# A 27,000-instruction transformer kernel on one core: mean one tile sooner, weight refills one by one at two mixers, sign-flipped logits, more background steps

## The chip, the core and the metric

The kernel runs on one core of a Trainium2 chip. TensorE (PE) multiplies 128-row tiles into PSUM, VectorE (DVE) and ScalarE (ACT) do elementwise work, GpSimd (POOL) a few elementwise operations, SyncE (SP) issues most DMAs. The metric is the device time of one execution in microseconds (us), median of several runs.

## What is computed

Two blocks, 256 tokens of width 1024, all in float32. The first puts 16 meta tokens in front (272 tokens) and runs two layers of SwiGLU, mixer, SwiGLU; the mixer is a neighborhood attention (16 heads), then a differential attention (8 heads). The second is a hybrid layer: causal attention (8 heads; with 256 tokens MoBA's own block is all there is) beside an mLSTM (4 heads), one output projection, then a squared-ReLU MLP.

```python
h = h + 0.5 * rmsnorm(swiglu(rmsnorm(h, g[0]), ...), g[1])
h = h + rmsnorm(mixer(rmsnorm(h, g[2])), g[3])
h = h + 0.5 * rmsnorm(swiglu(rmsnorm(h, g[4]), ...), g[5])
# differential attention, per head
p = softmax(q @ k.T + bias)              # two maps
o = rmsnorm((p[0] - lam * p[1]) @ v, subln_g) * (1 - lambda_init)
# hybrid layer
ig = mi + b_igate;  lf = log_sigmoid(mf + b_fgate)
hm = rmsnorm(mlstm(q, k, v, ig, lf)) * g * sigmoid(mo)
x = x + rmsnorm(concat(att, hm) @ w_out, g_mix_post)
x = x + rmsnorm(square(relu(rmsnorm(x) @ w_up)) @ w_down, g)
```

## The kernel before

**Products.** Activations lie transposed, features on partitions and tokens along the row, 8 blocks of 128 features. Every float32 product is made of three: x and w are split into a high half and a low half (the rest), and `mm3` (L387 to L389) multiplies xh·wh, xl·wh, xh·wl. `gemm` does that for the 8 blocks k of one output tile of 128 columns, 24 products; `inside` is a table of functions to be called after block k, and after the blocks in `bg_at[0]` it calls `bg()`, one step of a background generator.

**Weights.** `Weights` keeps a ring of 7 split tiles. `high` makes the high half on ACT (L150), `low` subtracts it on DVE (L162); a raw buffer holds two tiles, and its second `low` lets SP load the next. `pump(n)` does up to n lows (of tiles whose high half was ordered before) and n highs, as far as the ring has room. Engines run their instructions in the order in which the code was written, so a pump's place is its place in both queues.

**Phase start.** `start_phase` needs four weight tiles at once, multiplies them with an unnormalized x, sums the squares of h on DVE (`norm.sum`, L441 to L443), and ends with `pump(2)`. The factor 1/rms comes later: `Norm.steps` puts `head` (row sums on PE at L338, a small DVE row at L350, a power on POOL) after block 0 of the second tile behind the start, and `tail` (transposes, then ACT's copy `rb`, L456) after block 3. The first of these two tiles waits in PSUM as `p2`. Evacuations multiply by `rb`.

**Mixers.** `mixer` writes 20 such tiles behind the start, (value, then query, key, value for three groups), each followed by its evacuation, `W.pump()` and `bg()`, with `bg_at` at blocks 2 and 5. The background is an attention generator: per unit u `scores` (PE products, then `softmax` on DVE and ACT), `weights` (division by the sum), `turn` (transposes two units later), `turn_v` every second unit, `values`. Score and product tiles share six PSUM buffers, transposes have two. The hybrid layer has its own loop over `plan`, and three generators in turn: `gates`, `mlstm`, `causal_attention`. What is left of them at the end runs inside `proj_out`, two steps per block.

Of the kernel before, what the change touches and what calls it, by code (L numbers as in the profile page):

```python
# [20 lines left out]
NM = 16  # L21
# [182 lines left out]
def block_kernel(ctx: ExitStack, tc: tile.TileContext, a, out):  # L204
# [254 lines left out]
    def start_phase(norm, post, n=4):  # L459
# [43 lines left out]
        W.low_if()  # L503
        W.done(n)
        W.pump(2)
        return ps

    def first_phase(norm, feed, n=4):
# [69 lines left out]
        W.low()  # L578
# [4 lines left out]
        W.pump(2)  # L583
        W.pump(2)
# [52 lines left out]
    def ffn(norm, post, before, start=start_phase):  # L637
# [20 lines left out]
        for n in range(1, NF // 2):  # L658
            for q in range(2):
                p = ps_mm()  # L660
                if n == 1 and q == 0:
                    p2 = p
                    gemm(p, norm.x, c)
                    continue
                elif n == 1:
                    gemm(p, norm.x, c, inside=norm.steps)
# [239 lines left out]
    def softmax(ps, parts, n):  # L906

        lg, mx = tmp("lg"), -3.0e38
# [8 lines left out]
        return e, sm  # L917
# [32 lines left out]
    def na_attention():  # L950
# [8 lines left out]
        def scores(u):  # L959
# [5 lines left out]
            s0 = 2 - 2 * qt  # L965
            for b in range(2):
                hd = 2 * hp + b
                bias = bt[hp // 2][:, hd % 4, s0:s0 + 4, :].rearrange("p s k -> p (s k)")
                P[u, b] = softmax(ps[b], [(slice(0, NM), mb[:, hd * NM:hd * NM + NM]), (GRID, bias)], T)

        def weights(u):
            for b in range(2):
                e, sm = P[u, b]
                r = small([128, 1])
                dve.reciprocal(r, sm)
                dve.tensor_scalar(e, e, r, None, op0=OP.mult)
                P[u, b] = e
# [97 lines left out]
    def mixer(norm, post, evac, attention, q_cols, before):  # L1075
# [6 lines left out]
        for n, part, st in [(n,) + x for n, x in enumerate(  # L1082
                [(2, 0)] + [(part, st) for st in range(1, 4) for part in (0, 1, 2)])]:
            c = q_cols if part == 0 else norm.cols
            for q in range(2):
                before(2 * n + q)
                p = ps_mm()
                gemm(p, norm.x, c, inside=norm.steps if n == 0 and q else {})
                if n == 0 and q == 0:
                    p2 = p  # L1090
                    continue
# [8 lines left out]
                W.pump()  # L1100
# [68 lines left out]
    def da_attention():  # L1169
        vp, A, AT, OS, normed = {}, {}, {}, {}, {}  # L1170

        def scores(u):
            hd, qt = divmod(u, 2)
            A[u] = []
            for s in range(2):
# [4 lines left out]
                A[u].append(softmax(ps, [(ALL, t5b[hd // 4][:, hd % 4, u0:u0 + T])], T))  # L1180

        def weights(u):
            (e0, s0), (e1, s1) = A[u]
            r0, r1 = small([128, 1]), small([128, 1])
# [5 lines left out]
            A[u] = e0  # L1190
# [10 lines left out]
        def values(u):  # L1201
# [5 lines left out]
            m, r = small([128, 1]), small([128, 1])  # L1207
            dve.tensor_scalar(m, ss, 1.0 / 128, EPS, op0=OP.mult, op1=OP.add)
            pool.tensor_tensor(r, m, mhalf[:, 0:1], op=OP.pow)
            normed[u] = o, r  # L1210

        def scale(u):
            hd, qt = divmod(u, 2)
            o, r = normed.pop(u)
            if qt == 0:
                OS[hd] = keep()
            dve.tensor_scalar(OS[hd][:, qt * 128:qt * 128 + 128], o, r, None, op0=OP.mult)
# [74 lines left out]
    def gates():  # L1292
# [47 lines left out]
    def mlstm():  # L1340
# [57 lines left out]
        for u in range(8 + 4):  # L1398
# [17 lines left out]
            yield  # L1416

# [37 lines left out]
    def causal_attention():  # L1455
# [3 lines left out]
        def scores(u):  # L1459
# [3 lines left out]
            for b in range(2):  # L1463
                s = slice(64 * b, 64 * b + 64)
                pe.matmul(ps[b][:, 0:n], qk[s, hp, QT[qt]], qk[s, 4 + hp, NM:NM + n], start=True, stop=True)
            for b in range(2):
                lg, mx = tmp("lg"), small([128, 1])
                dve.tensor_tensor_reduce(out=lg[:, 0:n], in0=ps[b][:, 0:n], in1=causal[:, 256 - n:256], scale=1.0,
                                         scalar=-3.0e38, op0=OP.add, op1=OP.max, accum_out=mx)
                nmx = small([128, 1])  # L1470
                dve.tensor_scalar(nmx, mx, -0.125, None, op0=OP.mult)
                e, sm = keep(), small([128, 1])
                act.activation(e[:, 0:n], lg[:, 0:n], AF.Exp, bias=nmx, scale=0.125, accum_out=sm)
                P[u, b] = e, sm

        def weights(u):
            n = 128 * (u % 2 + 1)
            for b in range(2):
                e, sm = P[u, b]
                r = small([128, 1])  # L1480
                dve.reciprocal(r, sm)
                dve.tensor_scalar(e[:, 0:n], e[:, 0:n], r, None, op0=OP.mult)
# [44 lines left out]
    for n, (kind, i) in enumerate(plan):  # L1527
# [3 lines left out]
        gemm(p, norm.x, c, inside=norm.steps if n == 1 else {})  # L1531
        if n == 0:
            p2 = p
            continue
# [39 lines left out]
    for f in range(4, 32):  # L1574
        p = ps_mm()
        gemm(p, norm.x, c, inside=norm.steps if f == 5 else {})
        if f == 4:
            p2 = p
            continue
# [101 lines left out]
```

## Time and profile before

| | us |
|---|---|
| median of 3 runs | 1453.06 (1451.36 to 1454.84) |
| the profiled execution | 1454.09 |
| its span | 1452.3 |
| PE busy | 1422.2 (98%) |
| DVE busy | 927.7 (64%) |
| ACT busy | 753.2 (52%) |
| mean granted clock | 0.993 |

The first mixer lies at about 228 to 345 us, the second at 798 to 910, the hybrid layer's at 1121 to 1245. In a row of the timeline the first number is the start, the second how long the row took (rows of several instructions are merged), and the bracket says how long the engine stood idle before and what ended that.

### The profile page before, as it was taken

Reading aid. Unit: us, or ns where it says so; the run is one execution under the profiler, and the core shown is the slowest. Engines: PE = TensorE matmul, PEld = TensorE weight load, DVE = VectorE, ACT = ScalarE, POOL = GpSimd, SP = SyncE. Lnnn points to the kernel's source line nnn. Section 1 sums busy time; section 2 is a strip of 40 time slices with the busy share of each in tenths; the row PEclk is TensorE's granted clock in tenths of the full one; section 3 lists DMA queues with packets and bytes.
Section 4 is the critical chain, followed back from the end, with each engine's and each line's share of the span. In section 5 each row is a group of like instructions: output and inputs, shape, how many; then the busy total and the mean of one; then the engine's idle time right before and its main releaser. Section 6 shows DMA issues by size and latency. Waiting matters only on the chain.

```text
span 1452.3 us, 27152 instructions
## 1 busy us (share of the span) xinstructions
PE 1422.2 (98%) x11092; PEld 1365.1 (94%) x11092; DVE 927.7 (64%) x1852; ACT 753.2 (52%) x1331; POOL 154.3 (11%) x149
## 2 busy tenths in 40 slices
PE   9999999999999999999999899999999999999997
PEld 9999998788999999999999799999999888999886
DVE  6767448874775544865545777686644878686542
ACT  6554446665654444554444556564444565676541
POOL 1314000100021100121100011021200000000000
PEclk9999999999999999999999999999999999999999
DMA  8896555431475555365553433275554443265650
GB/s 267 259 254 181 184 167 138 110 117 59 140 254 174 168 189 167 117 204 174 177 172 117 145 117 116 88 232 177 192 190 140 142 149 116 88 213 195 211 180 29
DMA packets 230025, 236.40 MB, mean 163 GB/s; under 512 B 17857, under 2 KB 220390, under 8 KB 229710
## 3 DMA queue, kind: packets, MB, share of 16 engines
q1 hardware_dynamic: 228702, 229.36, 49.6%
q0 software_dynamic: 656, 4.94, 1.2%
q8 instruction: 87, 1.43, 0.4%
q10 hardware_dynamic: 544, 0.38, 0.1%
q14 instruction: 36, 0.29, 0.1%
HBM read 233.60 MB, written 5.13 MB: 164 GB/s over the span
## 4 chain that ended last, share of the span: by engine, by line
PE 71%; DVE 4%; ACT 1%; issue 0%; POOL 0%; DVEq 0%; POOLq 0%; ACTq 0%
PE pm L387 19%; PE pm L389 18%; PE pm L388 18%; PE ps L1604 2%; PE ps L1603 2%; PE ps L1605 2%; PE pm L500 2%; PE pm L496 1%; DVE wl L162 1%; PE pm L497 1%; PE ps L1205 1%; PE ps L1177 1%; PE pt L338 1%; DVE hb L615 0%; DVE xh L480 0%
## 5 line engine op out<-in xcount | busy, mean ns | idle before, releaser
L162 DVE TENSOR_TENSOR wl<-wr,wh 128x1024 fp32r<-128x1024 f32 (+1 forms) x430 | 516.2, 1208 | 119.5 <-ACT wh L150 118.7
L387 PE MATMUL pm<-xh,wh 128*128 128x272 f32 (+1 forms) x1992 | 583.8, 293 | 2.2 <-ACT ring L986 1.2
L389 PE MATMUL pm<-xh,wl 128*128 128x272 f32 (+1 forms) x1992 | 571.6, 287 | 0.0
L388 PE MATMUL pm<-xl,wh 128*128 128x272 f32 (+1 forms) x1992 | 570.2, 286 | 0.0
L150 ACT ACTIVATE wh<-wr 128x1024 fp32r<-128x1024 f32 (+1 forms) x430 | 441.0, 1033 | 196.9 <-PE pm L388 117.7
L387 PEld LDWEIGHTS pm<-xh,wh 128*128 128x128 f32 x1992 | 377.5, 190 | 15.8 <-issue 11.0
L388 PEld LDWEIGHTS pm<-xl,wh 128*128 128x128 f32 x1992 | 377.4, 189 | 0.1
L389 PEld LDWEIGHTS pm<-xh,wl 128*128 128x128 f32 x1992 | 377.4, 189 | 0.0
L389 PE MATMUL pm<-mh,wl 128*128 128x272 f32 (+1 forms) x704 | 202.3, 287 | 0.0
L387 PE MATMUL pm<-mh,wh 128*128 128x272 f32 (+1 forms) x704 | 202.1, 287 | 0.0
L388 PE MATMUL pm<-ml,wh 128*128 128x272 f32 (+1 forms) x704 | 201.6, 286 | 0.0
L648 POOL TENSOR_TENSOR sr<-sl,rb 128x272 f32<-128x272 f32 (+1 forms) x88 | 106.9, 1219 | 318.9 <-ACT sl L646 318.9
L389 PEld LDWEIGHTS pm<-mh,wl 128*128 128x128 f32 x704 | 132.7, 189 | 0.0
L387 PEld LDWEIGHTS pm<-mh,wh 128*128 128x128 f32 x704 | 132.6, 188 | 0.0
L388 PEld LDWEIGHTS pm<-ml,wh 128*128 128x128 f32 x704 | 132.6, 188 | 0.0
L414 ACT ACTIVATE mh<-m 128x272 fp32r<-128x272 f32 (+1 forms) x88 | 37.7, 429 | 122.8 <-DVE m L653 122.7
L653 DVE TENSOR_TENSOR m<-pm,sr 128x272 f32<-128x272 f32 (+1 forms) x88 | 38.3, 435 | 79.4 <-PE pm L389 75.5
L644 DVE TENSOR_TENSOR gq<-pm,rb 128x272 f32<-128x272 f32 (+1 forms) x88 | 37.6, 435 | 74.7 <-PE pm L389 66.8
L646 ACT ACTIVATE sl<-gq 128x272 f32<-128x272 f32 (+1 forms) x88 | 36.9, 427 | 92.3 <-DVE gq L644 92.0
L343 POOL TENSOR_TENSOR s<-s,mhalf 128x3 f32<-128x3 f32 (+1 forms) x15 | 11.9, 793 | 607.7 <-DVE s L356 356.6
L382 DVE TENSOR_TENSOR accf<-accf,sq 128x272 f32<-128x272 f32 (+1 forms) x42 | 18.3, 435 | 82.5 <-ACT sq L381 82.4
L916 ACT ACTIVATE keep<-lg,s 128x272 f32<-128x272 f32 x64 | 33.5, 523 | 48.2 <-DVE s L914 47.8
(337 smaller groups left out, 1801.8 us busy)
## 6 DMA issues: line engine op xcount, KB each, us to landing
wr<-in_ffn_w_gate_dram SPq DMA_DIRECT2D x43, 1024.0 KB
wr<-in_ffn_w_up_dram SPq DMA_DIRECT2D x43, 1024.0 KB
wr<-in_ffn_w_down_dram SPq DMA_DIRECT2D x32, 1024.0 KB
wr<-in_w_up_dram SPq DMA_DIRECT2D x16, 1024.0 KB
wr<-in_w_down_dram SPq DMA_DIRECT2D x16, 1024.0 KB
wr<-in_ffn_w_down_dram SPq DMA_DIRECT2D x16, 768.0 KB
wr<-in_na_w_qkv_dram SPq DMA_DIRECT2D x12, 1024.0 KB
wr<-in_da_w_qkv_dram SPq DMA_DIRECT2D x12, 1024.0 KB
```

The costliest lines, as they stand in the source:

```text
L150: self.nc.scalar.activation(hi, w, AF.Copy)
L162: engine.tensor_tensor(lo, w, hi.bitcast(F32), op=OP.subtract)
L387: pe.matmul(ps, wh[:, k, :], xh[:, j, cols], start=start, stop=False)
L388: pe.matmul(ps, wh[:, k, :], xl[:, j, cols], start=False, stop=False)
L389: pe.matmul(ps, wl[:, k, :], xh[:, j, cols], start=False, stop=stop)
L414: act.activation(hi, src, AF.Copy)
L500: pe.matmul(ps[q][:, c], w[q][0][:, k, :], norm.xl[:, k, c], start=False, stop=k == 7)
L644: dve.tensor_tensor(t[:, c], ps[:, c], norm.rb[:, c], op=OP.mult)
L646: act.activation(s[:, c], t[:, c], AF.Silu)
L648: pool.tensor_tensor(s2[:, c], s[:, c], norm.rb[:, c], op=OP.mult)
L653: dve.tensor_tensor(t[:, c], ps[:, c], gated.pop(f)[:, c], op=OP.mult)
L916: act.activation(e[:, 0:n], lg[:, 0:n], AF.Exp, bias=nmx, accum_out=sm)
```

## The change

In the `order` rows below numbers behind a name tell buffers apart.

*Mean sooner.* `head` moves to block 3 of the first tile behind a phase start (`norm.first`), `tail` to block 1 of the second. `start_phase` loses its second `low_if` and `pump(2)`; the callers pump after the first tile instead: 2 in the feed-forward phases and the hybrid layer, 1 in `mixer`. In `mixer` later tiles pump 1, and 2 only in the second tile of a step from the fourth step (n >= 3).

*Softmax.* The logits are written with the opposite sign and their minimum is taken, which serves as the exponential's bias with scale -1; the operation that negated the maximum goes. Both sums of a unit lie in one tile, and one reciprocal takes them. In the differential attention e0 is no longer scaled: e0 + e1·x with x = -lam·s0/s1, and 1/s0 enters in the row norm and in `scale`.

*Steps.* `gates` has two more `yield`s around the log-sigmoid, `mlstm` two before its last head.

```diff
-            self.steps = {0: self.head, 3: self.tail}
+            self.first, self.second = {3: self.head}, {1: self.tail}
...
         norm.sum(squares)
-        W.low_if()
         W.done(n)
-        W.pump(2)
         return ps
...
-        W.low()
         norm.sum(squares)
         for _ in range(n):
             W.next()
         W.done(n)
-        W.pump(2)
-        W.pump(2)
+        W.pump(1)
...
-            lo, mx = mx, small([128, 1])
-            dve.tensor_tensor_reduce(out=lg[:, cols], in0=ps[:, cols], in1=bias, scale=1.0, scalar=lo,
-                                     op0=OP.add, op1=OP.max, accum_out=mx)
-        nmx = small([128, 1])
-        dve.tensor_scalar(nmx, mx, -1.0, None, op0=OP.mult)
-        e, sm = keep(), small([128, 1])
-        act.activation(e[:, 0:n], lg[:, 0:n], AF.Exp, bias=nmx, accum_out=sm)
+            hi, mn = mn, small([128, 1])
+            dve.tensor_tensor_reduce(out=lg[:, cols], in0=ps[:, cols], in1=bias, scale=-1.0, scalar=hi,
+                                     op0=OP.add, op1=OP.min, accum_out=mn)
+        e = keep()
+        act.activation(e[:, 0:n], lg[:, 0:n], AF.Exp, bias=mn, scale=-1.0, accum_out=sm)
...
         def weights(u):
+            r = small([128, 2])
+            dve.reciprocal(r, P.pop(u))
             for b in range(2):
-                e, sm = P[u, b]
-                r = small([128, 1])
-                dve.reciprocal(r, sm)
-                dve.tensor_scalar(e, e, r, None, op0=OP.mult)
...
-                gemm(p, norm.x, c, inside=norm.steps if n == 0 and q else {})
+                gemm(p, norm.x, c, inside=(norm.first, norm.second)[q] if n == 0 else {})
                 if n == 0 and q == 0:
                     p2 = p
+                    W.pump(1)
                     continue
...
-                W.pump()
+                W.pump(2 if n >= 3 and q else 1)
...
-            dve.reciprocal(r0, s0)
-            dve.reciprocal(r1, s1)
-            dve.tensor_scalar(e0, e0, r0, None, op0=OP.mult)
-            dve.tensor_tensor(r1, r1, nlam, op=OP.mult)
-            dve.scalar_tensor_tensor(e0, e1, r1, e0, op0=OP.mult, op1=OP.add)
+            dve.reciprocal(r, sm)
+            dve.scalar_tensor_tensor(x, r[:, 1:2], sm[:, 0:1], nlam, op0=OP.mult, op1=OP.mult)
+            dve.scalar_tensor_tensor(e0, e1, x, e0, op0=OP.mult, op1=OP.add)
...
-            dve.tensor_scalar(m, ss, 1.0 / 128, EPS, op0=OP.mult, op1=OP.add)
+            dve.scalar_tensor_tensor(m, ss, r0, r0, op0=OP.mult, op1=OP.mult)
+            dve.tensor_scalar(m, m, 1.0 / 128, EPS, op0=OP.mult, op1=OP.add)
...
         yield
         yield
+        yield
         dve.scalar_tensor_tensor(f, f, 0.0, w[32:36, :], op0=OP.min, op1=OP.subtract)
+        yield
         yield
...
                 scale(u - 3)
             yield
+            if u == 10:
+                yield
+                yield
...
         if n == 0:
             p2 = p
+            W.pump()
             continue
```

DVE's queue in the first mixer, before, from the weights of unit 0 (reciprocals, scaling of the exponentials `keep`) over one tile's evacuation (`qkv`, product tile `pm` times `rb`) to the first logits of unit 1. `wl` is a weight tile's low half, `lg` the logits, `s` small tiles:

```order
L975 RECIPROCAL s_2916<-s_2896 128x1
L976 TENSOR_SCALAR keep_2569<-keep_2569,s_2916 128x272
L975 RECIPROCAL s_2919<-s_2905 128x1
L976 TENSOR_SCALAR keep_2569<-keep_2569,s_2919 128x272
L934 TENSOR_TENSOR qkv_2928<-pm_2875,rb_2825 128x272
L162 TENSOR_TENSOR wl_2865<-wr_2758,wh_2864 128x1024
L162 TENSOR_TENSOR wl_2871<-wr_2758,wh_2870 128x1024
L911 ISA lg_2945,s_2946<-ps_2941,mb 128x16
L911 ISA s_2946 128x1
L911 ISA lg_2945,s_2948<-ps_2941,bt_1139,s_2946 128x256
L911 ISA s_2948 128x1
L914 TENSOR_SCALAR s_2950<-s_2948 128x1
```

The same stretch now:

```order
L971 RECIPROCAL s_2901<-s_2879 128x2
L974 TENSOR_SCALAR keep_2569<-keep_2569,s_2901 128x272 x2
L930 TENSOR_TENSOR qkv_2911<-pm_2865,rb_2815 128x272
L162 TENSOR_TENSOR wl_2843<-wr_2508,wh_2842 128x1024
L909 ISA lg_2923,s_2924<-ps_2918,mb 128x16
L909 ISA s_2924 128x1
L909 ISA lg_2923,s_2926<-ps_2918,bt_1139,s_2924 128x256
L909 ISA s_2926 128x1
L909 ISA lg_2929,s_2930<-ps_2919,mb 128x16
```

One `wl` of the tile is gone, so is the `TENSOR_SCALAR s<-s` behind the logits, and one reciprocal of two columns stands where two stood.

DVE's queue at the gates of the hybrid layer, before, from the evacuation of the tile behind the gates' (`vt`) to the copy of the transposed gates (`gi`); `vtok` holds the gate rows here, and L1303 is the log-sigmoid's last step:

```order
L1427 TENSOR_TENSOR vt_13570<-pm_13804,rb_13827 128x256
L162 TENSOR_TENSOR wl_13768<-wr_13482,wh_13767 128x1024
L162 TENSOR_TENSOR wl_13771<-wr_13482,wh_13770 128x1024
L1303 SCALAR_TENSOR_TENSOR vtok_13571<-vtok_13571 4x256
L1427 TENSOR_TENSOR vt_13570<-pm_13863,rb_13827 128x256
L162 TENSOR_TENSOR wl_13855<-wr_13758,wh_13854 128x1024
L162 TENSOR_TENSOR wl_13861<-wr_13758,wh_13860 128x1024
L1308 COPY gi<-pt_13900 128x72
```

And now:

```order
L1431 TENSOR_TENSOR vt_13362<-pm_13603,rb_13613 128x256
L162 TENSOR_TENSOR wl_13595<-wr_13274,wh_13594 128x1024
L162 TENSOR_TENSOR wl_13601<-wr_13274,wh_13600 128x1024
L1431 TENSOR_TENSOR vt_13362<-pm_13655,rb_13613 128x256
L162 TENSOR_TENSOR wl_13647<-wr_13550,wh_13646 128x1024
L162 TENSOR_TENSOR wl_13653<-wr_13550,wh_13652 128x1024
L1303 SCALAR_TENSOR_TENSOR vtok_13363<-vtok_13363 4x256
L1431 TENSOR_TENSOR vt_13362<-pm_13692,rb_13613 128x256
L162 TENSOR_TENSOR wl_13683<-wr_13598,wh_13682 128x1024
L162 TENSOR_TENSOR wl_13689<-wr_13598,wh_13688 128x1024
L1309 COPY gi<-pt_13728 128x72
```

The log-sigmoid stands behind one more evacuation and two more low halves, and from it to the copy of `gi` the same three instructions stand.

PE's queue inside the hybrid layer's output projection, before, from the last scores of the causal attention (`ps<-qk`) on; `pm<-Oh` and `pm<-Ol` are the projection's products:

```order
L1465 MATMUL ps_15141<-qk_13569 128x256
L1465 MATMUL ps_15142<-qk_13569 128x256
L387 MATMUL pm_15006<-Oh_13567,wh_14570 128x256
L388 MATMUL pm_15006<-Ol_13568,wh_14570 128x256
L389 MATMUL pm_15006<-Oh_13567,wl_14571 128x256
L387 MATMUL pm_15007<-Oh_13567,wh_14648 128x256
L388 MATMUL pm_15007<-Ol_13568,wh_14648 128x256
L389 MATMUL pm_15007<-Oh_13567,wl_14649 128x256
L387 MATMUL pm_15008<-Oh_13567,wh_14698 128x256
```

And now, from the last scores on; `ps<-ring,vtok` are the values of the last but one pair of heads, `pt<-ident` transposes:

```order
L1469 MATMUL ps_14908<-qk_13361 128x256
L1469 MATMUL ps_14909<-qk_13361 128x256
L1503 MATMUL ps_14925<-ring_13560,vtok_13363 64x128 x6
L1338 MATMUL pt_14933<-ident,vt_13362 128x128 x2
L1494 MATMUL pt_14937<-ident,vtok_13363 128x128
L1494 MATMUL ps_14940<-ident,mq_13364 128x128
L387 MATMUL pm_14723<-Oh_13359,wh_14338 128x256
L388 MATMUL pm_14723<-Ol_13360,wh_14338 128x256
L389 MATMUL pm_14723<-Oh_13359,wl_14339 128x256
```

Twelve products followed the last scores before (seven stand here); now the values follow them. Further on the last values of all were followed by 24 products of this kind, 12 for another head pair and then 12 for their own; now by their own 12 alone.

## Rows read from the trace of the kernel before

**Rows 1.** The page, part 1: engine, busy us, share, instructions.

```profile
PE 1422.2 (98%) x11092; PEld 1365.1 (94%) x11092; DVE 927.7 (64%) x1852; ACT 753.2 (52%) x1331; POOL 154.3 (11%) x149
```

**Rows 2.** PE's waits: for whom, total us, times, longest.

```profile
PE pt L985 <- ACT bt L892: 3.3, 4, 2.2
...
PE ps L1015 <- DVE s L911: 1.9, 2, 1.3
PE pt L1391 <- DVE mq L1385: 1.8, 1, 1.8
...
PE pm L387 <- ACT ring L986: 1.2, 1, 1.2
```

**Rows 3.** Windows: length, PE busy, granted clock (1.00 is 2.4 GHz), DMA.

```profile
246.00:256.00 10.00, 6.89 (x45) 0.83 0.80 219
266.00:271.00 5.00, 2.79 (x21) 1.00 0.70 218
819.00:832.00 13.00, 7.86 (x39) 0.74 0.51 163
1000.00:1025.00 25.00, 25.00 (x213) 1.00 0.61 199
1149.00:1157.00 8.00, 7.28 (x39) 0.57 0.79 254
```

**Rows 4.** Timeline of PE, first mixer: scores of units 1 and 2.

```profile
242.42 0.73 PE L964 MATMUL ps<-kq 64*128 64x272 f32 x4
...
247.16 0.73 PE L964 MATMUL ps<-kq 64*128 64x272 f32 x4
```

**Rows 5.** Timeline of DVE, first mixer: one tile, with unit 1.

```profile
245.72 0.43 DVE L934 TENSOR_TENSOR qkv<-pm,rb 128x272 f32<-128x272 f32 x1
246.07 2.35 DVE L162 TENSOR_TENSOR wl<-wr,wh 128x1024 fp32r<-128x1024 f32 x2
248.34 0.17 DVE L911 CUSTOM_DVE_ANT_0 lg<-ps,mb 128x16 f32<-128x16 f32 x1
...
250.72 0.17 DVE L975 RECIPROCAL s<-s 128x1 f32<-128x1 f32 x1 [0.21 <-ACT keep L916]
...
251.19 0.43 DVE L934 TENSOR_TENSOR qkv<-pm,rb 128x272 f32<-128x272 f32 x1
```

**Rows 6.** Timelines of POOL and DVE: a bias mask and what lay beside it.

```profile
255.27 3.47 POOL L776 TENSOR_TENSOR bt<-bt,misc 128x1536 f32<-128x1536 f32 x1 [19.00 <-DMA bt<-rpb_rows]
...
255.97 2.84 DVE L1021 TENSOR_TENSOR lm<-lm,mx 16x64 f32<-16x64 f32 x1
```

**Rows 7.** Timeline of DVE, second mixer: one tile, with unit 1.

```profile
815.57 0.42 DVE L1155 SCALAR_TENSOR_TENSOR kq<-pm,rb 128x256 f32<-128x256 f32 x1
...
820.02 0.16 DVE L1186 RECIPROCAL s<-s 128x1 f32<-128x1 f32 x1 [0.38 <-ACT keep L916]
...
820.97 0.42 DVE L1155 SCALAR_TENSOR_TENSOR kq<-pm,rb 128x256 f32<-128x256 f32 x1
```

**Rows 8.** Timeline of PE, second mixer: scores of units 1, 2; values of 0.

```profile
813.34 0.73 PE L1177 MATMUL ps<-kq 64*128 64x272 f32 x4
...
817.44 0.73 PE L1177 MATMUL ps<-kq 64*128 64x272 f32 x4
...
825.72 1.65 PE L1205 MATMUL ps<-vs,ring 128*128 128x128 f32 x6 [5.14 <-ACT vs L891]
```

**Rows 9.** Timeline of PE, hybrid layer: gate transposes, cumulative sums.

```profile
1147.91 0.28 PE L1307 MATMUL pt<-ident,vtok 36*128 36x36 f32 x2 [2.22 <-DVE vtok L1303]
...
1150.78 0.56 PE L1311 MATMUL pt<-gi,misc 128*128 128x4 f32 x2 [0.72 <-DVE gi L1308]
```

**Rows 10.** Timeline of DVE, hybrid layer: log-sigmoid; last low half of attention.

```profile
1147.35 0.41 DVE L1303 SCALAR_TENSOR_TENSOR vtok<-vtok 4x256 f32<-4x256 f32 x1
...
1244.16 0.42 DVE L415 TENSOR_TENSOR Ol<-ps,Oh 128x256 fp32r<-128x256 f32 x1 [2.83 <-ACT Oh L414]
```

**Rows 11.** Timeline of PE, hybrid layer: the last values.

```profile
1242.83 0.88 PE L1501 MATMUL ps<-ring,vtok 128*64 128x128 f32 x12
```

More of the change, by code (lines that the diff above doesn't have):

```diff
@@ L662, in ffn @@
                     p2 = p
-                    gemm(p, norm.x, c)
+                    gemm(p, norm.x, c, inside=norm.first)
+                    W.pump(2)
                     continue
                 elif n == 1:
-                    gemm(p, norm.x, c, inside=norm.steps)
+                    gemm(p, norm.x, c, inside=norm.second)
                     gate(ps4[0], 0)
@@ L965, in scores @@
             s0 = 2 - 2 * qt
+            sm = small([128, 2])
             for b in range(2):
@@ L968, in scores @@
                 bias = bt[hp // 2][:, hd % 4, s0:s0 + 4, :].rearrange("p s k -> p (s k)")
-                P[u, b] = softmax(ps[b], [(slice(0, NM), mb[:, hd * NM:hd * NM + NM]), (GRID, bias)], T)
+                P[u, b] = softmax(ps[b], [(slice(0, NM), mb[:, hd * NM:hd * NM + NM]), (GRID, bias)], T, sm[:, b:b + 1])
+            P[u] = sm
         def weights(u):
+            r = small([128, 2])
+            dve.reciprocal(r, P.pop(u))
             for b in range(2):
-                e, sm = P[u, b]
-                r = small([128, 1])
-                dve.reciprocal(r, sm)
-                dve.tensor_scalar(e, e, r, None, op0=OP.mult)
-                P[u, b] = e
+                e = P[u, b]
+                dve.tensor_scalar(e, e, r[:, b:b + 1], None, op0=OP.mult)
         def turn(u):
@@ L1169, in da_attention @@
     def da_attention():
-        vp, A, AT, OS, normed = {}, {}, {}, {}, {}
+        vp, A, AT, OS, normed, sums, first = {}, {}, {}, {}, {}, {}, {}
         def scores(u):
@@ L1174, in scores @@
             A[u] = []
+            sums[u] = small([128, 2])
             for s in range(2):
@@ L1179, in scores @@
                 u0 = 128 * (1 - qt)
-                A[u].append(softmax(ps, [(ALL, t5b[hd // 4][:, hd % 4, u0:u0 + T])], T))
+                A[u].append(softmax(ps, [(ALL, t5b[hd // 4][:, hd % 4, u0:u0 + T])], T, sums[u][:, s:s + 1]))
         def weights(u):
-            (e0, s0), (e1, s1) = A[u]
-            r0, r1 = small([128, 1]), small([128, 1])
-            dve.reciprocal(r0, s0)
-            dve.reciprocal(r1, s1)
-            dve.tensor_scalar(e0, e0, r0, None, op0=OP.mult)
-            dve.tensor_tensor(r1, r1, nlam, op=OP.mult)
-            dve.scalar_tensor_tensor(e0, e1, r1, e0, op0=OP.mult, op1=OP.add)
-            A[u] = e0
+            e0, e1 = A[u]
+            sm, r, x = sums.pop(u), small([128, 2]), small([128, 1])
+            dve.reciprocal(r, sm)
+            dve.scalar_tensor_tensor(x, r[:, 1:2], sm[:, 0:1], nlam, op0=OP.mult, op1=OP.mult)
+            dve.scalar_tensor_tensor(e0, e1, x, e0, op0=OP.mult, op1=OP.add)
+            A[u], first[u] = e0, r[:, 0:1]
         def turn(u):
@@ L1465, in scores @@
                 pe.matmul(ps[b][:, 0:n], qk[s, hp, QT[qt]], qk[s, 4 + hp, NM:NM + n], start=True, stop=True)
+            sm = small([128, 2])
             for b in range(2):
[L1467 to L1473, printed above, removed]
+                lg, mn, e = tmp("lg"), small([128, 1]), keep()
+                dve.tensor_tensor_reduce(out=lg[:, 0:n], in0=ps[b][:, 0:n], in1=causal[:, 256 - n:256],
+                                         scale=-0.125, scalar=3.0e38, op0=OP.add, op1=OP.min, accum_out=mn)
+                act.activation(e[:, 0:n], lg[:, 0:n], AF.Exp, bias=mn, scale=-1.0, accum_out=sm[:, b:b + 1])
                 P[u, b] = e, sm
@@ L1477, in weights @@
             n = 128 * (u % 2 + 1)
+            r = small([128, 2])
+            dve.reciprocal(r, P[u, 0][1])
             for b in range(2):
[L1479 to L1482, printed above, removed]
+                e = P[u, b][0]
+                dve.tensor_scalar(e[:, 0:n], e[:, 0:n], r[:, b:b + 1], None, op0=OP.mult)
                 P[u, b] = e
@@ L1530, in block_kernel @@
         p = ps_mm()
-        gemm(p, norm.x, c, inside=norm.steps if n == 1 else {})
+        gemm(p, norm.x, c, inside=(norm.first, norm.second)[n] if n < 2 else {})
         if n == 0:
             p2 = p
+            W.pump()
             continue
@@ L1575, in block_kernel @@
         p = ps_mm()
-        gemm(p, norm.x, c, inside=norm.steps if f == 5 else {})
+        gemm(p, norm.x, c, inside=(norm.first, norm.second)[f - 4] if f < 6 else {})
         if f == 4:
             p2 = p
+            W.pump(2)
             continue
```

14 lines of the change are left out of this document (7 added, 7 removed).

## The prediction

> **What bounds the kernel now.** First the page's busy times: TensorE (PE) is busy 1422.2 of 1452.3 us [rows 1], so nothing that VectorE (DVE) or ScalarE (ACT) saves counts unless PE waits for it. Then who made PE wait, longest first: apart from start and end the waits are a dozen, nearly all in the three mixers [rows 2]. Then the granted clock, in windows laid round those waits: PE runs at 2.4 GHz but for three stretches at 1.2, each right after a wait. A share of 0.83 over 10 us, 0.74 over 13 and 0.57 over 8 [rows 3] lacks 1.7, 3.4 and 3.4 us of full clock. Not every wait costs that: 2.2 us near 267 left the clock at 1.00 [rows 2, 3]. Last the timelines round each wait, for what came late.
>
> *First mixer.* PE reaches the scores of units 1 and 2 (one per tile) at 242.42 and 247.16, 4.74 us apart [rows 4]. DVE needs 5.47 from one evacuation (245.72) to the next (251.19), and starts on the scores of unit 1 at 248.34, 5.92 after PE began them [rows 5]. So DVE falls behind until the PSUM slots of the scores are all taken: 1.9 at L1015 and 1.2 at L387 [rows 2].
>
> *Second mixer.* The same with 5.40 [rows 7] against 4.10, until the values of unit 0 wait 5.14 us for the V tile, whose copy stands on ACT behind unit 2's exponentials [rows 8].
>
> *Third mixer.* PE comes to the gate transposes before DVE has the log-sigmoid (2.22), then to the cumulative sum before their copy (0.72) [rows 9]; later the last mLSTM head waits for its scale, 1.8 [rows 2].
>
> **The change part by part.** Times are against the profiled execution, 1454.09 us, 1.03 above the median of the runs, 1453.06.
>
> *One refill per tile in the first two mixers.* Before, two weight tiles were split per turn until the ring was full; now one, and two only in every second turn from the fourth step. DVE loses one subtraction per tile: two take 2.27 from 246.07 to the next instruction [rows 5], one 1.13.
>
> *Logits, weights.* The sign flip takes a [128,1] operation out of each softmax: two per unit, which I take as 0.15 together, half of a reciprocal each [rows 5]. But the merged reciprocal waits for both sums. Before, the second reciprocal already stood waiting 0.21 for its sum (250.72). That sum comes 0.15 earlier, so the merged one starts at 250.57, and with its own 0.20 and two scalings of 0.27 the unit ends at 251.31 instead of 251.19 [rows 5]: 0.12 later, not earlier. First mixer's tile: 5.47 - 1.13 + 0.12 = 4.46, under PE's 4.74. In the second the unscaled weights also drop one scaling: the reciprocal starts at 820.02 - 0.15 = 819.87, then 0.2 + 0.2 + 0.42, end 820.69 instead of 820.97 [rows 7]. Tile: 5.40 - 1.13 - 0.28 = 3.99, under 4.10. Bounds of these small steps: -0.3 and +0.3 per tile.
>
> *The mean one tile sooner.* Same row sums and transposes, moved; the reciprocal root's row comes two k-steps earlier, six products of 25.00/213 = 0.117 us [rows 3], so 0.7. PE never waited for it; it lets DVE begin 0.7 earlier. In the other phase starts nothing waits on it, before or after, so zero there; a sum that is not ready in time would cost some 0.3, two or three products, in each of eight starts, 2.4, which stays in the range. The refills that move behind it at the kernel's start leave PE two split tiles in hand, 24 products of 0.117 each; zero too.
>
> *First mixer, sum.* DVE starts 0.7 sooner, has one refill fewer before unit 0 (1.13) and 1.01 less in the tile: unit 1's lag is 5.92 - 2.84 = 3.1 us instead of 5.92, so the slot for which PE stood 1.9 us from 247.9 is free before it comes, and ACT's copies behind it come as much earlier. Waits -3.1, clock -1.7. The 2.2 at L985 [rows 2] I leave standing: it hangs on how far DVE lags three units on.
>
> There the two bias masks on GpSimd fall. L1021 took 2.84 us on DVE just while a mask of 3.47 ran, its three other executions being far shorter; it spans that mask's end [rows 6]. The change moves the masks' loads in SP's order, so the masks strike other instructions; the two holds of some 2.6 us are in the time now and I take them as unchanged; bounds -2.2 (the L985 wait goes) and +2.6 (one more is exposed). The Trainium skill, "SBUF — State Buffer", section "SBUF: two separate sides", says that DVE and GpSimd share one port pair under a lock held for a whole instruction; the trace agrees (2.84 beside 3.47). By that rule a DVE with its weights only one tile ahead would pass a hold on to PE, where a full ring hid it.
>
> *Second mixer, sum.* Unit 2's logits came 6.1 after its scores (lag of two tiles, by the same reckoning). Saved: 0.7, 1.13, and twice 1.41: 4.7. So the V copy is there at 825.72 - 4.7 = 821.0, and PE, which came at 820.58 [rows 8], waits some 0.5 instead of 5.14: -4.6. Clock -3.4, of which I leave 0.2 for the part that may lie in the wait itself: -3.2. At the tail each scale gets one more [128,1] operation, 0.16 [rows 7], exposed twice: +0.3.
>
> *Third mixer.* Two added steps move the gate transposes one tile (24 products, 2.82) later on PE, and the operation they wait for behind one more evacuation (0.35) and two refills (2.27) on DVE. It ran at 1147.35 [rows 10]; now 1147.35 - 0.7 + 2.62 = 1149.27, and PE can start 0.56 after it, as before: 1149.83. PE arrives at 1147.91 - 2.22 + 2.82 = 1148.51: it waits 1.3. The sums wait for the copy behind the same three instructions as before, 3.43 after the log-sigmoid (1147.35 to 1150.78): 1152.70. PE gets there 0.2 + 12 x 0.117 = 1.6 after 1149.83, so it waits 1.25. Together 2.6 instead of 2.94: -0.3. Since no single wait is as long as 1.4, below the 2.2 that passed unpunished, I take the fall of the clock as gone: 3.4 less the 0.36 that lay in the wait, -3.0; it is the least sure term, and its other end is 0.
>
> The two steps before the last head let PE issue 15 more products (1.76) and two rotations first: -1.8. In return attention ends later within the output projection. Before, the last values (1242.83) were followed by 12 products for another head while DVE made the low half, ready at 1244.58 [rows 10, 11]; now the products that need it come at once, at 1243.7. That shows 0.9. Between the last scores and their transposes 12 products (1.4) are gone too; how much of them was slack no row tells, between none and all is exposed, and I take 0.4: in all +1.3, bounds 0 and +3.
>
> *Sum.* -3.1 - 1.7 - 4.6 - 3.2 + 0.3 - 0.3 - 3.0 - 1.8 + 1.3 = -16.1: 1438.0 for the profiled execution, 1437.0 for the median.
>
> **The rivals.**
> *Waits thinned, not gone.* The masks' hold comes through (+2.6), the third mixer's clock still falls (+3.0) and its tail costs 3 instead of 1.3 (+1.7): 1437.0 + 7.3 = 1444. For it: two waits of 1.3 lie 1.6 apart there, and the split weights' lead over PE, counted in the code, is one or two tiles for the first eight, where it grew to six within four before. Against: the lag falls to 3 us, less than a tile.
> *Only the work that left DVE is given back.* PE's waits are then moved, not removed: each of the first two mixers gains one tile's saving, 1.0 and 1.4, and the third 0.3, the falls stay: 1450. Against: both lags fall under a tile.
> *Slower: PE waits for the low half of the weights in every early tile.* With a lead of one tile a DVE tile longer than PE's shows at once. If the merged reciprocal's wait keeps it at 5.4 in spite of the refill, PE loses 0.7 and 1.3 us in each of eight tiles, 16, in place of the 7.7 of waits that go; the falls stay, the third mixer gives 3.8: 1453.06 + 16 - 7.7 - 3.8 = 1458. It decides once a tile costs DVE over 4.74 in the first mixer or 4.10 in the second. For it: in the second the reckoned margin is 0.11. Against: rows 5 and 7 put the wait inside the sums above.
>
> **How the numbers follow.** Forecast 0.58, thinned waits 0.26, work only 0.08, slower 0.08. What a measurement of this kernel tells from no change is about 0.2%, 2.9 us. The forecast, the thinned waits and a part of the third case, which lies on that bound, are faster by more: 0.87; the rest of the third, 0.05, is within; slower 0.08. The forecast's own range is 1431 to 1443, down to what L985 and smaller waits could give. For 8 in 10: 1430 to 1447, which leaves out the two last cases and a little below.
>
> **What would show it.** L1015, the ring copy and L1205 gone from PE's waits or under 1 us; clock share 1.00 round 250 and 825; PE waits of 1.3 and 1.25 one tile later at the gates, with the clock at 1.00 after them; no wait at the last mLSTM transpose; one of about 1 us for the low half at the end of attention. Wrong would be: PE waiting at L389 for a low half in the early tiles of a mixer, a DVE tile over 4.74, or the clock falling at the gates again.

## The result and the profile after

The changed kernel takes 1440.22 us (median of 4 runs, 1439.65 to 1441.22) against 1453.42 beside it (4 runs, 1451.36 to 1454.84): ratio 0.9911, interval 0.9894 to 0.9928. The forecast was 1437.0 within 1430 to 1447. The profiled execution took 1440.03 us, its span 1437.9, 14.4 less than before's 1452.3.

First, where the 14.4 lies. Each norm begins with transposes of its factors (`pt<-ident,s`); those that the change doesn't move cut the span into stages. The windows of PE between them hold the first mixer, feed-forward, the second mixer, feed-forward, the hybrid mixer, and the rest (length, PE busy, count, granted clock, DMA share, GB/s). Before:

```profile
216.82:375.55 158.73, 150.21 (x1269) 0.99 0.39 115
375.55:786.79 411.24, 411.11 (x3256) 1.00 0.54 174
786.79:930.88 144.09, 137.65 (x1057) 0.98 0.35 114
930.88:1123.12 192.24, 192.09 (x1620) 1.00 0.55 179
1123.12:1260.07 136.95, 131.86 (x1040) 0.98 0.40 127
1260.07:1452.30 192.23, 184.41 (x1187) 0.99 0.49 160
```

The same stages of the changed kernel:

```profile
216.93:369.22 152.29, 147.79 (x1268) 1.00 0.41 119
369.22:780.10 410.88, 410.76 (x3257) 1.00 0.54 174
780.10:917.27 137.17, 134.77 (x1056) 1.00 0.37 120
917.27:1109.35 192.08, 191.92 (x1619) 1.00 0.56 179
1109.35:1246.25 136.90, 130.48 (x1040) 1.00 0.41 127
1246.25:1437.90 191.65, 184.27 (x1187) 0.99 0.50 160
```

The first mixer is 6.44 us shorter, the second 6.92, the third 0.05, all else together 1.0. Length less busy is what PE stands idle: in the third mixer 5.09 us before and 6.42 now. So two mixers gained nearly all, and the third, forecast at -3.8, nothing.

PE's waits now, which answer to [rows 2] (for whom, total us, times, longest):

```profile
PE pm L387 <- DVE Ol L415: 2.1, 1, 2.1
PE pt L1222 <- DVE keep L1216: 1.9, 2, 1.3
PE pt L1308 <- DVE vtok L1303: 1.2, 1, 1.2
PE pt L1451 <- ACT vtok L1339: 1.1, 1, 1.1
PE pt L982 <- ACT bt L889: 1.1, 2, 0.6
...
PE pt L1312 <- DVE gi L1309: 1.0, 1, 1.0
PE pt L1451 <- ACT mv L1329: 0.8, 1, 0.8
...
PE ps L1203 <- ACT vs L888: 0.3, 1, 0.3
```

The first mixer's 1.9 for slots of the scores and 1.2 for the ring are gone, and the 5.14 at the first values (now L1203) is 0.3. The wait for `Ol` at L387, 0.97 before, is 2.1, and two at the rotation's transposes (L1451) are new.

The windows that answer to [rows 3], round the same work in the three mixers, have the clock at 1.00:

```profile
246.00:256.00 10.00, 9.86 (x89) 1.00 0.79 166
806.00:819.00 13.00, 12.71 (x96) 1.00 0.46 153
1137.00:1145.00 8.00, 6.70 (x57) 1.00 0.88 278
```

DVE's timeline, as [rows 5, 7], from one evacuation to the next:

```profile
243.62 0.44 DVE L930 TENSOR_TENSOR qkv<-pm,rb 128x272 f32<-128x272 f32 x1
...
247.86 0.43 DVE L930 TENSOR_TENSOR qkv<-pm,rb 128x272 f32<-128x272 f32 x1
...
806.49 0.42 DVE L1153 SCALAR_TENSOR_TENSOR kq<-pm,rb 128x256 f32<-128x256 f32 x1
...
810.46 0.42 DVE L1153 SCALAR_TENSOR_TENSOR kq<-pm,rb 128x256 f32<-128x256 f32 x1
```

A tile is 4.24 us in the first mixer (forecast 4.46) and 3.97 in the second (3.99). PE's own, between its scores as in [rows 4, 8], are 4.54 and 4.10, so DVE no longer falls behind.

PE's timeline at the gates, as [rows 9], and the wait behind them:

```profile
1135.99 0.28 PE L1308 MATMUL pt<-ident,vtok 36*128 36x36 f32 x2 [1.25 <-DVE vtok L1303]
...
1138.86 0.36 PE L1312 MATMUL pt<-gi,misc 128*128 128x4 f32 x2 [0.97 <-DVE gi L1309]
...
1149.05 0.67 PE L1451 MATMUL pt<-raw,misc 128*128 128x256 f32 x2 [0.83 <-ACT mv L1329]
```

1.25 and 0.97 were forecast as 1.3 and 1.25; the 0.83 was not forecast.

### The profile page after: what moved, and what is told of

It is laid out like the page before. It is cut to its first block, busy times and chain, and to the rows that moved or that the text cites. A ratio compares the mean times of both kernels' runs of the same rounds, so it can differ in the third digit from the quotient of the medians.

```text
span 1437.9 us, 27029 instructions
## 1 busy us (share of the span) xinstructions
PE 1415.2 (98%) x11092; PEld 1358.9 (95%) x11092; DVE 912.9 (63%) x1732; ACT 754.4 (52%) x1333; POOL 162.0 (11%) x149
## 4 chain that ended last, share of the span: by engine, by line
PE 90%; DVE 6%; ACT 2%; issue 1%; POOL 0%; DVEq 0%; POOLq 0%; ACTq 0%
PE pm L387 24%; PE pm L389 23%; PE pm L388 23%; PE ps L1608 2%; PE ps L1607 2%; PE ps L1609 2%; DVE wl L162 2%; PE pm L500 2%; PE pm L496 2%; PE pm L497 1%; PE ps L1203 1%; PE pt L338 1%; ACT keep L912 1%; PE ps L991 1%; PE pm L534 1%
## 5 line engine op out<-in xcount | busy, mean ns | idle before, releaser
L387 PE MATMUL pm<-xh,wh 128*128 128x272 f32 (+1 forms) x1992 | 580.9, 292 | 2.2 <-DVE Ol L415 2.1
L387 PEld LDWEIGHTS pm<-xh,wh 128*128 128x128 f32 x1992 | 375.5, 189 | 15.0 <-issue 10.4
L387 PE MATMUL pm<-mh,wh 128*128 128x272 f32 (+1 forms) x704 | 202.1, 287 | 0.0
L387 PEld LDWEIGHTS pm<-mh,wh 128*128 128x128 f32 x704 | 132.5, 188 | 0.0
L343 POOL TENSOR_TENSOR s<-s,mhalf 128x3 f32<-128x3 f32 (+1 forms) x15 | 19.1, 1276 | 592.9 <-DVE s L356 336.1
L496 PE MATMUL pm<-xh,wh 128*128 128x272 f32 (+1 forms) x224 | 56.7, 291 | 0.6
```

The source lines that it names most:

```text
L387: pe.matmul(ps, wh[:, k, :], xh[:, j, cols], start=start, stop=False)
L496: pe.matmul(ps[q][:, c], w[q][0][:, k, :], norm.xh[:, k, c], start=k == 0, stop=False)
```

## The experiments

Twelve kernels were run. "Before" beside them was 1453.5 us for e1 to e4, 1455.3 for e5 to e8 and 1454.6 for the rest, so ratios are compared. Stage lengths of the profiled executions repeat within 0.15 us where no wait and no clock changes; a star marks a stage with a stretch at 1.2 GHz.

| kernel | median us | ratio to before, 95% | first mixer | second | third |
|---|---|---|---|---|---|
| before | 1453.42 | 1 | 158.73* | 144.09* | 136.95* |
| changed | 1440.22 | 0.9911 (0.9894-0.9928) | 152.29 | 137.17 | 136.90 |
| e1 refill by two | 1448.91 | 0.9964 (0.9950-0.9979) | 155.89 | 141.76* | 136.86 |
| e2 gates short | 1437.13 | 0.9889 (0.9875-0.9904) | 153.35* | 137.19 | 135.09 |
| e3 last head short | 1439.42 | 0.9906 (0.9891-0.9921) | 153.40* | 137.16 | 136.89 |
| e4 mask in eight | 1438.08 | 0.9895 (0.9878-0.9911) | 151.71 | 137.18 | 136.88 |
| e5 changed again | 1439.27 | 0.9901 (0.9884-0.9919) | 151.81 | 137.13 | 136.78 |
| e6 softmax as before | 1444.04 | 0.9931 (0.9914-0.9948) | 155.52* | 137.58 | 136.76 |
| e7 gates short, mean late | 1443.51 | 0.9929 (0.9914-0.9943) | 154.30* | 138.07 | 137.62* |
| e8 low half first | 1436.89 | 0.9882 (0.9866-0.9897) | 149.83 | 137.15 | 136.77 |
| e9 refill alone | 1443.47 | 0.9923 (0.9908-0.9938) | 154.84 | 138.47 | 135.55* |
| e10 low first, gates short | 1435.47 | 0.9870 (0.9855-0.9884) | 150.05 | 137.16 | 135.02 |
| e11 low first, no steps | 1435.34 | 0.9869 (0.9855-0.9884) | 150.18 | 137.17 | 134.01 |
| e12 low first, one step | 1434.85 | 0.9862 (0.9845-0.9878) | 149.93 | 137.15 | 134.59 |

**e1, refills by two again in the first two mixers.**

```diff
                     p2 = p
-                    W.pump(1)
+                    W.pump(2)
...
-                W.pump(2 if n >= 3 and q else 1)
+                W.pump()
```

> The changed kernel, but in the first two mixers weights are again split two tiles per turn (the refill behind the first product tile too). Theory, the single refill carries most of the gain in these two mixers: VectorE's tile grows by one subtraction of 1.13 us, from 4.24 to about 5.4 in the first mixer and from 3.97 to about 5.1 in the second, above TensorE's 4.54 and 4.10; the waits for the scores' slots and for the V copy come back with about 2.4 and 3.4 us, and the granted clock falls once more in the second mixer (about 3): 1449 us, between 1446 and 1451. Rival, the earlier mean and the shorter softmax are enough by themselves: the lag stays under a tile, no wait over 1 us at the scores or at the first values, clock 1.00 in both: 1440 to 1442.

The theory's 1449 was met: 1448.91. DVE's tile is 5.37 and 5.11 us, as its timeline shows, in the first and in the second mixer:

```profile
244.81 0.44 DVE L930 TENSOR_TENSOR qkv<-pm,rb 128x272 f32<-128x272 f32 x1
...
250.18 0.44 DVE L930 TENSOR_TENSOR qkv<-pm,rb 128x272 f32<-128x272 f32 x1
...
811.30 0.42 DVE L1153 SCALAR_TENSOR_TENSOR kq<-pm,rb 128x256 f32<-128x256 f32 x1
...
816.41 0.42 DVE L1153 SCALAR_TENSOR_TENSOR kq<-pm,rb 128x256 f32<-128x256 f32 x1
```

PE's timeline at the first values of the second mixer:

```profile
820.93 0.94 PE L1203 MATMUL ps<-vs,ring 128*128 128x128 f32 x6 [3.81 <-ACT vs L888]
```

PE's window round it:

```profile
820.00:827.00 7.00, 6.07 (x34) 0.76 0.47 150
```

One subtraction per tile (1.13) decides whether the V copy (ACT's copy `vs`, L888) is 0.3 or 3.8 us late, and behind the 3.8 this execution ran at half clock for a while (0.76 over 7 us). The third mixer stays.

**e2, the gates without the two added steps; e3, the last mLSTM head without its two.**

```diff
         yield
         yield
-        yield
         dve.scalar_tensor_tensor(f, f, 0.0, w[32:36, :], op0=OP.min, op1=OP.subtract)
         yield
-        yield
```

> The changed kernel without the two added steps around the log-sigmoid. Theory, these steps alone took away the fall of the clock: TensorE waits 2.2 and 0.7 us at the gates again and runs some 7 us at half clock behind them, which costs 3.3; of the waits behind the gates in the changed kernel (0.33 and 0.83) nothing is left: 1440.2 - 0.4 + 3.3 = 1443 us. Rival, the fall had come from VectorE's backlog, which the other edits cut as well: the waits of 2.2 and 0.7 come back but the clock stays at 1.00: 1440 us.

```diff
             yield
-            if u == 10:
-                yield
-                yield
```

> The changed kernel without the two added steps before the last mLSTM head. Theory, these steps only moved a wait: the 1.8 us at the last head's transposes comes back, the 1.14 at the rotation's transposes near 1204 and the 1.5 at the end of the attention (0.52, 0.53, 0.48) go: 1439 to 1440 us, the same within the measurement. Rival, the forecast's reckoning: 1.8 back, 1.3 given back at the end, and the 1.14 near 1204 belongs to something else and stays: 1440.7. Second rival, the end of the attention doesn't depend on these steps: 1442.

In e2 neither theory foresaw the gate waits, and the time, 1437.13, lies below both (1443 and 1440). PE's timeline there:

```profile
1132.87 0.28 PE L1306 MATMUL pt<-ident,vtok 36*128 36x36 f32 x2 [1.48 <-DVE vtok L1302]
...
1135.73 0.36 PE L1310 MATMUL pt<-gi,misc 128*128 128x4 f32 x2 [1.00 <-DVE gi L1307]
```

PE's window round and behind it:

```profile
1133.00:1141.00 8.00, 7.00 (x59) 1.00 0.86 263
```

Without the steps the first wait is 1.48, not 2.2, and the clock does not fall; so the steps were not what kept it up. They lengthen the third mixer by 1.8 us (136.90 against 135.09). In e3 the sums are as the theory had them: a wait of 2.11 at the attention's transposes comes, the 1.14 and 1.05 of the end's 1.53 go, and the stage is the same, 136.89.

**e4, each of the two bias masks as eight additions.**

```diff
-        pool.tensor_tensor(t, t, window.unsqueeze(1).to_broadcast([128, 24, 64]), op=OP.add)
+        m = 24 if g < 2 else 3
+        for x in range(0, 24, m):
+            pool.tensor_tensor(t[:, x:x + m], t[:, x:x + m], window.unsqueeze(1).to_broadcast([128, m, 64]), op=OP.add)
```

> The changed kernel, but the two bias masks that GpSimd adds during the first mixer are eight additions of 128x192 each instead of one of 128x1536. Theory, VectorE is held for as long as one GpSimd addition lasts: the scaling that took 3.77 us (two instructions) beside a mask of 3.46 falls to 0.7 to 1.7, the evacuation behind it comes 2 to 3 us earlier, and TensorE's waits of 0.45 and 2.11 near 273 go: 1437.6 us. Rival, the hold is a sharing of bandwidth, so that eight small additions delay VectorE by the same 3 us in all: the waits stay and the time is 1440 us.

The timeline of DVE in the changed kernel, at the second mask (two scalings in one row):

```profile
268.16 3.77 DVE L974 TENSOR_SCALAR keep<-keep,s 128x272 f32<-128x272 f32 x2
```

The timeline of POOL beside it, the mask:

```profile
268.03 3.46 POOL L773 TENSOR_TENSOR bt<-bt,misc 128x1536 f32<-128x1536 f32 x1 [15.25 <-DMA bt<-rpb_rows]
```

The same two scalings in e4:

```profile
267.98 1.00 DVE L976 TENSOR_SCALAR keep<-keep,s 128x272 f32<-128x272 f32 x2
```

And e4's POOL, four of the small additions in a row:

```profile
266.29 2.26 POOL L775 TENSOR_TENSOR bt<-bt,misc 128x192 f32<-128x192 f32 x4 [7.81 <-DMA bt<-rpb_rows]
```

Half of the theory holds: DVE is held until the GpSimd instruction beside it ends, and 3.77 falls to 1.00. In the changed kernel the first scaling ends 0.17 behind the mask (271.66 after 271.49), in e4 0.16 behind the one piece beside it (268.70 after 268.54). The Trainium skill ("SBUF — State Buffer", section "SBUF: two separate sides") has the hold last for a whole instruction, and both traces agree. That piece is the last of its four, so how DVE fares between two pieces isn't shown here. But the 2.1 at L387 stayed at 2.04 and so was not the hold's, and the 0.45 at the scores of the meta tokens (L1012) is gone in e5 too, without any edit. Most of the hold was slack: in e4 DVE stands 1.91 at the next evacuation (270.88) until PE's tile is done. The time is no different from e5 within the intervals.

**e5, the changed kernel again; e6, softmax, weights and row norm of the first two mixers as before; e7, gates short and the mean late; e8, low halves ahead of the refills.** e5 has no edit.

> The changed kernel once more, word for word, beside the next three on the same chip: 1440 us, and the same waits of TensorE, apart from the granted clock behind waits of about 2 us, which theory lets fall in some executions and not in others. Rival: the clock behind each wait is always the same.

The edit of e6 is the change's diff of `softmax`, `scores`, `weights`, `values` and `scale` in those two mixers taken back, as here in the first one's weights:

```diff
-            r = small([128, 2])
-            dve.reciprocal(r, P.pop(u))
             for b in range(2):
-                e = P[u, b]
-                dve.tensor_scalar(e, e, r[:, b:b + 1], None, op0=OP.mult)
+                e, sm = P[u, b]
+                r = small([128, 1])
+                dve.reciprocal(r, sm)
+                dve.tensor_scalar(e, e, r, None, op0=OP.mult)
```

> The changed kernel with the softmax, the weights and the row norm of the first two mixers as they were before (maximum and its negation, a reciprocal for each sum, both exponentials scaled), the single refill kept. Theory, the refill does the work and these edits little: VectorE's tile goes from 4.24 to 4.1 to 4.4 in the first mixer, from 3.97 to 4.2 to 4.5 in the second, so that the first V copy is late by 0.3 to 1.2 us instead of 0.3, and the tail of the second mixer gets its 0.7 back: 1439.5 to 1441. Rival, the second mixer needs both, its margin being 0.13 under TensorE's 4.10: a wait of 2 us or more at the first values, the clock falls there: 1444 to 1446.

```diff
-            self.first, self.second = {3: self.head}, {1: self.tail}
+            self.first, self.second = {}, {0: self.head, 3: self.tail}
```

> The changed kernel without the two steps around the log-sigmoid and with the mean's sums at their old place in every phase start. Theory, it was the earlier mean that took 0.7 us from the wait at the gates and with it the fall of the clock: TensorE waits 2.2 at the gates again instead of 1.5, the clock falls for some 7 us behind it, and the first values of the second mixer wait 1.0 instead of 0.3: 1437.1 + 0.7 + 3.3 + 0.7 = 1442. Rival, the mean has no part in it: waits of 1.5 and 1.0 at the gates, clock 1.00: 1437.

```diff
+                W.flush()
                 W.pump(2 if n >= 3 and q else 1)
```

> The changed kernel, but in the first two mixers the low halves that wait to be made (Ol) are put into VectorE's queue ahead of the turn's weight refills instead of behind them. Theory, the 2.11 us near 274 is a PSUM slot: the values' tile holds it until its low half is subtracted behind two refills of 2.3 us; now the wait is under 0.3 and the other waits stay: 1438 us. Rival, the named release is a coincidence and TensorE waits for the weights that ScalarE splits at the same time: the wait stays near 2: 1440 us.

e5 has the waits of the changed kernel over 0.25 us again, without the 0.45 at the meta scores; its one fall of the clock lies just behind the first mixer.

e6 came out at the rival's number, 4.8 us slower than e5, but not where the rival put it. DVE's tile is 4.34 in the first mixer and 4.27 in the second, so the second mixer's lateness was sized rightly (first values wait 1.13, stage 0.45 longer). The loss is in the first mixer, 3.7 us: the ring is waited for again (0.60), L982 waits 1.11 instead of 0.59, several waits under 0.6 return, and this execution's clock fell behind the 2.11, where e5's did not. PE's busy time there is 149.46 against 147.74, so 1.7 of the 3.7 is clock and 2.0 are waits, though DVE's tile (4.34) is still shorter than PE's (4.54).

e7 shows what the earlier mean is worth. PE's timeline at the gates:

```profile
1137.11 0.28 PE L1306 MATMUL pt<-ident,vtok 36*128 36x36 f32 x2 [2.18 <-DVE vtok L1302]
```

PE's window behind them:

```profile
1138.00:1146.00 8.00, 7.67 (x41) 0.57 0.81 259
```

The wait is 2.18 instead of e2's 1.48 and the clock falls as before (0.57 in both). The two gate waits together are the same, 2.51 (2.18 and 0.33) against 2.48 (1.48 and 1.00): the earlier mean only shifts 0.7 from the first to the second, and what it gives there is the clock, 132.62 us of PE busy in the third mixer against 129.73. In each of the first two mixers PE waits 0.6 once for a low half of the weights, the sign of the slower rival; these stages are 0.95 and 0.88 longer than e2's. The first values of the second mixer wait 0.29, not the 1.0 foreseen.

e8 settles the 2.1. PE's timeline in the changed kernel:

```profile
274.70 0.39 PE L387 MATMUL pm<-xh,wh 128*128 128x272 f32 x1 [2.11 <-DVE Ol L415]
```

DVE's timeline there:

```profile
272.20 2.34 DVE L162 TENSOR_TENSOR wl<-wr,wh 128x1024 fp32r<-128x1024 f32 x2
274.47 0.51 DVE L415 TENSOR_TENSOR Ol<-ps,Oh 128x32 fp32r<-128x32 f32 x2
```

DVE's timeline in e8:

```profile
270.40 0.50 DVE L415 TENSOR_TENSOR Ol<-ps,Oh 128x32 fp32r<-128x32 f32 x2
270.83 2.34 DVE L162 TENSOR_TENSOR wl<-wr,wh 128x1024 fp32r<-128x1024 f32 x2
```

With the subtraction of `Ol` queued ahead of the refills no wait at that L387 is left, and the first mixer takes 149.83 instead of 151.81. The product that waited reads no `Ol`; what PE stood for was a PSUM slot: scores, values and product tiles share six, and the values' tile was free only when DVE, behind two refills (2.3 us together), had made its low half.

**e9, the refills alone; e10 to e12, low halves first with fewer steps.** e9 undoes softmax, mean and steps, and keeps the refills. e10 joins e2 and e8, e11 also takes e3's edit, e12 is e10 with one step:

```diff
         dve.scalar_tensor_tensor(f, f, 0.0, w[32:36, :], op0=OP.min, op1=OP.subtract)
         yield
+        yield
```

> The kernel before with the changed refills alone: softmax, weights and row norm as before in all three mixers, the mean's sums late, no added steps. Theory, the three edits of the first two mixers are needed together, because each only brings the lag of VectorE nearer to a tile: the waits for the ring and the V copy come back in part, those at the gates are 2.2 and 0.7 with the fall of the clock, and TensorE waits some 0.6 for a low half once in each mixer: 1440 + 4.8 + 6.4 (as the two runs without one edit each lost) = 1451 us, between 1448 and 1453. Rival, the refill alone carries the mixers, and only the gates are lost: 1445.

> The changed kernel without the two steps around the log-sigmoid and with the low halves ahead of the refills in the first two mixers. Theory, the two gains add, since they lie in different mixers: 1439.3 less 2.1 for the slot's wait and less 0.7 to 3 for the steps: 1434 to 1436.5 us; waits of 1.5 and 1.0 at the gates with the clock at 1.00. Rival, the clock falls at the gates in most executions when the wait is 1.5: 1438.

> The same, and without the two steps before the last mLSTM head: no added step is left. Theory, the steps only moved waits: a wait of 1.7 to 2.1 us near 1200 stays in one form or another and the end of attention loses its waits of 0.5: within 1 us of the kernel with these steps. Rival, they are worth the 1.8 us of the forecast: 1.8 slower.

> As the kernel with low halves first and short gates, but with one added step, between the log-sigmoid and its transposes. Theory, TensorE reaches the transposes 12 products (1.4 us) later, so that the wait of 1.5 falls to 0.1; the copy stays behind the same evacuation and refills, so the cumulative sums wait 1.0 to 1.4; everything behind moves half a tile, not a whole one, so the 0.83 at the rotation is not there: 0.5 to 1.5 us faster than without the step. Rival, the half tile brings new waits of the same size, as the whole one did: no difference.

In e9 the theory missed and the rival was near: 1443.47, a ratio of 0.9923. The windows of its three mixers:

```profile
215.47:370.31 154.84, 148.20 (x1269) 1.00 0.40 117
...
781.60:920.07 138.47, 135.09 (x1056) 1.00 0.37 118
...
1112.29:1247.84 135.55, 130.89 (x1040) 0.99 0.41 128
```

The refills alone give 3.9, 5.6 and 1.4 us of the three stages, some 11 of the 14 in all; so the other edits are no condition for it. These are all of the change's refills, those at the phase starts too, and 0.97 of the third mixer's 1.4 is a shorter time at half clock in this execution (PE busy 130.89 against 131.86). Losses from taking single edits out (8.7 in e1, 4.8 in e6, 6.4 in e7 against e2) add up to more than the gain; in part that is the clock, which in some of these executions also fell where it had not.

e10 is 1435.47: the two gains add. The third mixer's window in e11:

```profile
1106.91:1240.92 134.01, 129.23 (x1040) 1.00 0.42 130
```

Without any added step the third mixer is 1.0 shorter still than e10's 135.02; the time is the same within its interval, and in the profiled execution of e11 a stretch at half clock near 366, which e10's has not, takes the 1.0 back. e12 loses the 1.50 of e10's gates as foreseen, and the 1.72 at the last head's transposes as well; it keeps 0.96 and gets 0.59 and three of 0.25 to 0.39 instead. PE stands 1.54 less there but is busy 1.11 longer: 0.4 us better in the stage. The three cannot be told apart by time (1434.85 to 1435.47). All are faster than the changed kernel by their ratios, 0.986 to 0.987 against 0.9901 and 0.9911; e12's interval, the lowest, ends below both of the changed kernel's.

## Why the prediction was right, and where it was not

| step | forecast us | measured us |
|---|---|---|
| first mixer, waits and clock | -4.8 | -6.44 |
| second mixer, waits and clock | -7.5 | -6.92 |
| third mixer | -3.8 | -0.05 |
| everywhere else | 0 | -0.99 |
| sum, profiled execution's span | -16.1 | -14.40 |

*The refill and DVE's tile.* Right, and the main cause: one subtraction out of a tile is 1.13, measured by e1 as 5.37 - 4.24 and 5.11 - 3.97. The softmax edits together, reckoned at +0.12 in the first mixer, measured -0.10 (4.24 against e6's 4.34); in the second -0.30 (3.97 against 4.27), reckoned at -0.28.

*First mixer.* The waits at L1015 and for the ring went, and PE's busy time fell by 2.42, where 1.7 was put down to the clock. The 2.2 at L985, left standing, fell to 0.59, so the lag reached three units further than I followed it. In its place the slot of the values' tile, 0.97 before, cost 2.11. Of the mask's bound (+2.6) 0.45 came in the first profile and nothing in e5.

*Second mixer.* The V copy was forecast 0.5 late and is 0.29. The tail's scale was sized too low: +0.3 against the waits' +0.74, since the added operation stands in a chain. DVE's two operations ahead of the power and the wait for it last 889.87 to 891.00, 1.13 us, where one operation and the wait took 0.81 before.

*Third mixer: the step that failed.* "I take the fall of the clock as gone", -3.0, was put down to the added steps with -0.3 and -1.8 beside it. Three things were wrong. First, the fall went with the earlier mean, which takes 0.7 us off the gate wait (2.18 in e7, 1.48 in e2); I had counted it at the moved place alone and not asked what it does without the steps. Second, the steps push all that follows by a whole tile, into the rotation: 0.83 at L1451 is new (the 0.33 at L1321 is there in e2, e9 and e11 too, without the steps), the last head's 1.79 came back as 1.14 at another transpose, and the end costs 1.53 (forecast 1.3). Third, the 1040 instructions were busy 1.38 less, not 3.0; without steps, as in e11, they are busy 129.23, which is 2.6 less. So the clock gave back some 2.6 (2.9 by e7 against e2), and the steps made PE busy for 1.25 longer at the same clock; why isn't shown. The steps cost 2.9 us in this stage (136.90 against e11's 134.01), where the forecast gave them a gain of 3.8.

*The rest.* Zero was put for the mean in the other phase starts: the two stretches between the mixers gave 0.36 and 0.16, that behind the third 0.58. The 0.36 is the mean's: e9, where it is late, has 411.29 there, e6, where it is early, 410.86. The 0.58 is not: before, e6 and e9, with the old softmax in the first two mixers, have 192.1 to 192.2 there and all others 191.6 to 191.8; by what path isn't shown. The slower rival, PE waiting for low halves in the early tiles, shows with 0.6 once in each of the first two mixers in e7 and e9, where the mean is late, and not at all in the changed kernel.

The total was near by luck: the first mixer, better by 1.6 than forecast, and the rest, by 1.0, paid for part of the second, worse by 0.6, and the third, worse by 3.8.

## What to carry to other kernels

Where one engine feeds another by tiles, compare their times per tile: one operation of 1.13 us decided whether a lag of a tile built up, and with the other refills it was worth more than all other edits here. A shorter tile is not all, as e6's first mixer shows. An added pause moves every later step as well, so it has to be priced at the next place where the moved work meets other work, and tried alone. Work that frees a shared slot belongs ahead of refills that nobody waits for yet.

## What the runs showed of the hardware

The half clock is not decided by the length of one wait. The same wait of 2.11 us at L387 is followed by full clock in e5 and by half clock in e2. The window round it in e5:

```profile
272.00:277.00 5.00, 4.15 (x33) 1.00 0.65 210
```

And in e2:

```profile
272.00:277.00 5.00, 4.41 (x24) 0.68 0.67 210
```

And in e5 the clock fell at the end of a wait of 0.42 (L362, behind a norm's row sums), where it had not, behind the same wait, in the changed kernel's first profile:

```profile
366.00:371.00 5.00, 4.58 (x26) 0.66 0.51 167
```

So a stretch at half clock in one profiled execution, which cost 1.0 us (behind e11's first mixer, 411.91 against e10's 410.87) to 2.9 (the third mixer of e7), need not be a property of the kernel, and an argument that a wait "passed unpunished" has only one execution behind it. The mean clock of every run tells more: e7's four have 0.994 to 0.995 and e2's 0.997 to 0.999, so what e7 lost was not one execution's chance.

The opening differs as well between executions of the same code: PE's first products of the first feed-forward start at 9.98 in e2 and at 12.01 in e6. The timeline of e2:

```profile
9.98 0.39 PE L534 MATMUL pm<-xh,wh 128*128 128x272 f32 x1 [0.86 <-DVE wh L116]
```

The timeline of e6:

```profile
12.01 1.27 PE L534 MATMUL pm<-xh,wh 128*128 128x272 f32 x8 [0.76 <-DVE wh L116]
```

That is 2 us, more than most edits here are worth; stage lengths are free of it.
